# Shared buffers, weights and activations begin at many offsets modulo 512 bytes instead of one

## The chip, the cores and the metric

The kernel runs on one core of a Trainium2 chip (trn2). The metric is the device time of one execution, in microseconds (us). PE is TensorE, DVE VectorE, ACT ScalarE, POOL GpSimd, SP the engine that issues most DMAs; PEld is PE's weight load, which the profile keeps as a row of its own. SBUF is the on-chip memory of 128 partitions; an offset here is a byte offset within a partition, the same in all 128.

## The reference, cut to what matters

Two transformer blocks over 256 positions of width 1024, in float32. The first is a macaron block (feed-forward, mixer of gated linear attention and a gated convolution, feed-forward), the second takes the first one's output, 256 positions of context and a conditioning vector (feed-forward over both, a mixer of a bidirectional mLSTM and a spatial gate, feed-forward).

```python
def first_block(x, ...):
    x = x + 0.5 * swiglu(rmsnorm(x, ffn1_norm[l]), ffn1_w_gate[l], ffn1_w_up[l], ffn1_w_down[l])
    x = x + hybrid_mixer(rmsnorm(x, mix_norm[l]), w_in[l], w_a2[l], b_a[l], gla_out_norm[l], conv_w[l], w_out[l])
    x = x + 0.5 * swiglu(rmsnorm(x, ffn2_norm[l]), ffn2_w_gate[l], ffn2_w_up[l], ffn2_w_down[l])
    return rmsnorm(x, final_norm)

def ffn_sublayer(h, shift, scale, gate, g, w_in, w_out):      # second block
    hn = modulate(rmsnorm_2(h, g), shift, scale)
    a, b = jnp.split(hn @ w_in, 2, axis=-1)
    y = (jax.nn.silu(a) * b) @ w_out
    return h + 0.5 * gate[:, None, :] * y
```

Nearly all of the arithmetic is in the products `hn @ w`: widths 1024 to 2816, some 258 MB of weights read once.

## The kernel before, in words

**Split precision.** A float32 product is made of three products in float32r, a format that PE takes at one column a cycle. Each operand is split into a high part (rounded to float32r, on ACT) and a low part (the rest, on DVE); `mm3` (L142) and `mm3r` (L147) issue high x high, high x low and low x high into one PSUM accumulator. `split` (L116) does it for a weight tile: 512 KB come by DMA into `raw` (4 buffers of 4,096 bytes a partition), ACT writes `wh`, DVE writes `wl` (5 buffers each, pool `wsp`). Activations are normed, transposed by PE against the identity `ident` and split into `XH` and `XL` (16,384 bytes each, pool `const`) by `to_xT` (L175). The hidden activations of a feed-forward (`hT`), values, keys, queries, gates and other long-lived arrays live in 18 shared buffers, S0 to S17 (pool `slots`, tags handed out by `salloc`, L58, and given back by `sfree`); a buffer is as large as its largest tenant, 4,096 or 4,608 bytes.

**The order of the work.** PE follows the program: for each weight tile, all token tiles. In an input projection (`proj_chunk`, L259) the activations XH and XL are the stationary operand (128 columns, 512 bytes, loaded ahead of each product) and the weights wh, wl the moving one (512 columns). In a down projection (`ffn2tok`, L329, `ffn4tok`, L445) the stationary operand is a slice of a shared buffer. Where the result is wanted transposed (`projT`, L307, and `projT2`, L316: the query and key projections, the gate-up projections of the last two feed-forwards) the weights are stationary and XH, XL move, 512 or 256 columns. The first block's query-key projection (L587 to L595) takes its weight tile in slices of 272 and 256 columns; the attention of the second block (L993 to L996) moves values `VH` of 4 heads with 258 columns each, from a shared buffer.

SP issues the loads of the weights in the program's order, some tiles ahead, as far as raw buffers are free; ACT and DVE split as far as wh and wl are free. The modulation vectors of the second block (`ada_gen`, L532) are worked in between by DVE.

**Where things begin.** Pools follow one another in SBUF, and within a pool one tag after the other, each tile's size rounded up to 32 bytes. `pad` (L54) allocates a tile that nothing reads or writes. With the pads of the kernel before (96 elements ahead of `ident`, L1117; 32 after `tri`, L1132; 96 in pool `rp`, L1323) these all begin at 0 modulo 512: ident, XH, XL, the residuals x2 and x3, the temporaries t2, the rows bc, all 18 shared buffers, raw, wh, wl. Every 128-column slice then begins at 0 as well, and every 512- or 256-column slice but those of the two projections with 272 and 258 columns. The small table `cst` begins at 160, `mc` (the modulation sums) at 288, `tri` at 32.

```python
    def salloc(self, shape, dt=F32):
        i = self.free_slots.pop(0)
        ...
            t = self.slots.tile(shape, dt, tag=f"S{i}", name=self.nm(f"S{i}"))
```

Of the kernel before, what the change touches and what calls it, by code (L numbers as in the profile page):

```python
# [14 lines left out]
P = 128  # L15
D = 1024
# [7 lines left out]
class Kern:  # L24
    def __init__(self, tc, A, out, pools):
        self.tc, self.nc, self.A, self.out = tc, tc.nc, A, out
        self.__dict__.update(pools)
        self.n = 0
        self.free_slots = list(range(NSLOT))
        self.slot_of = {}  # L30
        self.filler = None
        self.fill_every = 0
        self.fill_count = 0
        self.filled = 0
        self.pre = []
        self.deferred = []
        self.later_pe = []
        self.held = 0


    def nm(self, s):
# [15 lines left out]

    def salloc(self, shape, dt=F32):  # L58
        i = self.free_slots.pop(0)
        if len(shape) == 3 and shape[1] * shape[2] > D:  # L60
            t = self.slots.tile([P, D + P], dt, tag=f"S{i}", name=self.nm(f"S{i}"))
            t = t[:, :shape[1] * shape[2]].rearrange("p (a b) -> p a b", a=shape[1])
        else:
            t = self.slots.tile(shape, dt, tag=f"S{i}", name=self.nm(f"S{i}"))
        self.slot_of[id(t)] = (i, t)
        return t

# [48 lines left out]
    def split(self, raw, n, dst=None):  # L116
        if dst is not None:
            wh, wl = dst
        else:
            wh = self.wsp.tile([P, 1024], F32R, tag="wh", name=self.nm("wh"))  # L120
            wl = self.wsp.tile([P, 1024], F32R, tag="wl", name=self.nm("wl"))
        if self.held:
            self.held -= 1
            with self.tc.issue_after(self.last[0].ins), self.tc.issue_after(self.last[1].ins):
                self.split_out(wh[:, :n], wl[:, :n], raw[:, :n])
        else:
            self.split_out(wh[:, :n], wl[:, :n], raw[:, :n])
        if self.fill_every:
            self.fill_count += 1
            if self.fill_count % self.fill_every == 0 and next(self.filler, 0) is None:  # L130
                self.filled += 1
        return wh, wl
# [979 lines left out]
    def run(self):  # L1112
# [3 lines left out]
            x[t] = self.xres.tile([P, D], F32, tag=f"x{t}", name=f"x{t}")  # L1116
        self.pad(self.cpool, 96)  # L1117
        self.ident = self.cpool.tile([P, P], F32, tag="ident", name="ident")
        self.XH = self.cpool.tile([P, 8, 512], F32R, tag="XH", name="XH")
        self.XL = self.cpool.tile([P, 8, 512], F32R, tag="XL", name="XL")  # L1120
        make_identity(nc, self.ident)
        g = {"f1": self.bc.tile([P, D], F32, tag="bc", name="bc_f1")}
        pre = []
# [332 lines left out]
```

## Time and profile before

| | us |
|---|---|
| runs before: median of 2 (lowest to highest) | 1410.33 (1409.53 to 1411.13) |
| the profiled execution | 1408.26 |
| its span, first to last instruction | 1406.5 |
| granted TensorE clock, mean | 0.998 of 2.4 GHz |
| PE busy, weight loads busy | 1384.6, 1169.7 |
| DVE, ACT, POOL busy | 919.1, 627.3, 30.4 |

The durations below come from the profiled execution, so a sum is made against 1408.26; the timed runs stand 2 us above it in the median. In a row of PE, `acc<-wh,XH` names the accumulator, the moving operand and the stationary one, in this order; `128x512` is 128 partitions by the moving columns. "Mean ns" of a product is from its start to its end and overlaps with its neighbours; the pace is the distance of the starts. A product of a shared buffer bears the name S without its number.

### The profile page before, as it was taken

Reading aid. Unit: us, or ns where it says so; the run is one execution under the profiler, and the core shown is the slowest. Engines: PE = TensorE matmul, PEld = TensorE weight load, DVE = VectorE, ACT = ScalarE, POOL = GpSimd, SP = SyncE. Lnnn points to the kernel's source line nnn. Section 1 sums busy time; section 2 is a strip of 40 time slices with the busy share of each in tenths; the row PEclk is TensorE's granted clock in tenths of the full one; section 3 lists DMA queues with packets and bytes.
Section 4 is the critical chain, followed back from the end, with each engine's and each line's share of the span. In section 5 each row is a group of like instructions: output and inputs, shape, how many; then the busy total and the mean of one; then the engine's idle time right before and its main releaser. Section 6 shows DMA issues by size and latency. Waiting matters only on the chain. (4 is left out here: it accounts for less than half of the span.)

```text
span 1406.5 us, 18795 instructions
## 1 busy us (share of the span) xinstructions
PE 1384.6 (98%) x7222; PEld 1169.7 (83%) x7222; DVE 919.1 (65%) x1308; ACT 627.3 (45%) x914; POOL 30.4 (2%) x49
## 2 busy tenths in 40 slices
PE   7999999999999999999999999999999999999997
PEld 6778888788888898888888887889888887899986
DVE  6898556878998475543555547377886567655545
ACT  5445447465446442322122224354865455444442
POOL 0000000000000000000000001001010000000000
PEclk9999999999999999999999999999999999999999
DMA  8888646447887664643665543334235666465662
GB/s 287 295 267 280 214 134 218 136 155 269 297 282 255 208 208 139 197 150 103 191 213 179 162 139 104 115 98 148 84 120 192 198 196 217 141 180 184 185 208 69
DMA packets 73307, 260.71 MB, mean 185 GB/s; under 512 B 8172, under 2 KB 9216, under 8 KB 73216
## 3 DMA queue, kind: packets, MB, share of 16 engines
q1 hardware_dynamic: 72928, 259.11, 57.0%
q8 instruction: 57, 0.93, 0.3%
q10 hardware_dynamic: 288, 0.39, 0.1%
q14 instruction: 34, 0.28, 0.1%
HBM read 258.32 MB, written 1.14 MB: 184 GB/s over the span
## 5 line engine op out<-in xcount | busy, mean ns | idle before, releaser
L77 DVE TENSOR_TENSOR wl<-raw,wh 128x1024 fp32r<-128x1024 f32 (+1 forms) x381 | 459.2, 1211 | 319.6 <-ACT wh L74 315.5
L74 ACT ACTIVATE wh<-raw 128x1024 fp32r<-128x1024 f32 (+1 forms) x381 | 398.9, 1051 | 575.7 <-PE acc L87 448.4
L87 PE MATMUL acc<-wh,XH 128*128 128x512 f32 (+2 forms) x816 | 273.6, 393 | 0.5 <-ACT t L74 0.4
L87 PE MATMUL acc<-wl,XH 128*128 128x512 f32 (+2 forms) x816 | 268.9, 388 | 1.5 <-DVE wl L77 1.3
L87 PE MATMUL acc<-wh,XL 128*128 128x512 f32 (+2 forms) x816 | 269.5, 388 | 0.2 <-DVE XL L77 0.2
L87 PE MATMUL acc<-wh,S 128*128 128x512 f32 x872 | 234.2, 391 | 0.2 <-DVE t L80 0.2
L87 PE MATMUL acc<-XH,wh 128*128 128x512 f32 (+1 forms) x776 | 199.7, 337 | 0.0
L87 PE MATMUL acc<-XL,wh 128*128 128x512 f32 (+1 forms) x776 | 199.4, 337 | 0.0
L87 PE MATMUL acc<-XH,wl 128*128 128x512 f32 (+1 forms) x776 | 199.3, 337 | 0.0
L87 PEld LDWEIGHTS acc<-wh,S 128*128 128x128 f32 x872 | 162.8, 188 | 35.7 <-DVE t L80 0.9
L551 DVE SCALAR_TENSOR_TENSOR S<-raw,S 128x1024 f32<-128x1024 f32 x112 | 136.8, 1222 | 68.8 <-DMA raw<-in_w_ada 67.9
L87 PEld LDWEIGHTS acc<-wl,XH 128*128 128x128 f32 x816 | 151.4, 188 | 33.3 <-DVE wl L77 3.9
L87 PEld LDWEIGHTS acc<-wh,XL 128*128 128x128 f32 x816 | 151.8, 188 | 31.1 <-DVE XL L77 1.1
L87 PEld LDWEIGHTS acc<-wh,XH 128*128 128x128 f32 x816 | 151.2, 188 | 30.9 <-ACT t L74 0.6
L87 PEld LDWEIGHTS acc<-XL,wh 128*128 128x128 f32 x776 | 133.8, 190 | 15.3
L87 PEld LDWEIGHTS acc<-XH,wh 128*128 128x128 f32 x776 | 133.7, 190 | 15.4
L87 PEld LDWEIGHTS acc<-XH,wl 128*128 128x128 f32 x776 | 133.8, 190 | 15.3
L87 PE MATMUL acc<-wl,S 128*128 128x512 f32 x436 | 131.5, 389 | 0.0
L87 PEld LDWEIGHTS acc<-wl,S 128*128 128x128 f32 x436 | 81.9, 188 | 16.9
L74 ACT ACTIVATE S<-t 128x512 fp32r<-128x512 f32 (+2 forms) x58 | 31.5, 544 | 48.2 <-DVE t L77 48.2
L74 ACT ACTIVATE XH<-tr 128x512 fp32r<-128x512 f32 x44 | 26.0, 596 | 41.0 <-PE tr L160 40.7
L160 PE MATMUL tr<-ident,t 128*128 128x128 f32 x200 | 32.1, 285 | 10.5 <-DVE t L77 9.4
(165 smaller groups left out, 894.9 us busy)
## 6 DMA issues: line engine op xcount, KB each, us to landing
raw<-in_gu SPq DMA_DIRECT2D x176, 512.0 KB, 4.3
raw<-in_d SPq DMA_DIRECT2D x88, 512.0 KB, 4.3
raw<-in_w_ada SPq DMA_DIRECT2D x72, 512.0 KB, 4.4
raw<-in_w_in SPq DMA_DIRECT2D x68, 512.0 KB, 4.2
raw<-in_w_qk SPq DMA_DIRECT2D x16, 512.0 KB, 3.5
bc<-modd SPq DMA_DIRECT2D x10, 512.0 KB, 4.6
raw<-in_w_out SPq DMA_DIRECT2D x8, 512.0 KB, 3.5
raw<-in_w_b SPq DMA_DIRECT2D x8, 512.0 KB, 4.1
```

The source lines that it names most:

```text
L74: return self.nc.scalar.activation(out=out, in_=in_, func=func, **kw)
L77: return self.nc.vector.tensor_tensor(out=out, in0=a, in1=b, op=op)
L87: self.nc.tensor.matmul(out, l, r, start=start, stop=stop, **kw)
L160: self.nc.tensor.transpose(tr[:, j, :], src[:, j * P:(j + 1) * P], self.ident)
L551: nc.vector.scalar_tensor_tensor(out=junk, in0=raw, scalar=1.0, in1=cb[r], op0=ALU.mult, op1=ALU.mult, accum_out=mc[:, o:o + 1])
```

## The change

Three pads are put around XH and XL in pool `const` (64 elements ahead of XH, 48 ahead of XL, 16 behind it: 256, 192 and 64 bytes, in all 512), one of 8 elements (32 bytes) between the buffers of wh and those of wl, and every shared buffer is allocated as a flat tile of 16 + 1024 or 16 + 1152 elements, of which the tenant takes a view. So XH begins at 256 modulo 512, XL at 448; behind them nothing changes modulo 512 up to the shared buffers; S0 begins at 0 and each next one 64 bytes further (modulo 512), so that the eighteen go twice and a little more round the eight multiples of 64; raw and wh begin at 128, wl at 160. No instruction is added or removed.

```diff
     def salloc(self, shape, dt=F32):
         i = self.free_slots.pop(0)
-        if len(shape) == 3 and shape[1] * shape[2] > D:
-            t = self.slots.tile([P, D + P], dt, tag=f"S{i}", name=self.nm(f"S{i}"))
-            t = t[:, :shape[1] * shape[2]].rearrange("p (a b) -> p a b", a=shape[1])
-        else:
-            t = self.slots.tile(shape, dt, tag=f"S{i}", name=self.nm(f"S{i}"))
+        n = math.prod(shape[1:])
+        t = self.slots.tile([shape[0], 16 + (D if n <= D else D + P)], dt, tag=f"S{i}", name=self.nm(f"S{i}"))[:, :n]
+        if len(shape) == 3:
+            t = t.rearrange("p (a b) -> p a b", a=shape[1])
+        elif len(shape) == 4:
+            t = t.rearrange("p (a b c) -> p a b c", a=shape[1], b=shape[2])
         self.slot_of[id(t)] = (i, t)
         return t
...
             wh = self.wsp.tile([P, 1024], F32R, tag="wh", name=self.nm("wh"))
+            if not self.padded:
+                self.pad(self.wsp, 8)
+                self.padded = True
             wl = self.wsp.tile([P, 1024], F32R, tag="wl", name=self.nm("wl"))
...
         self.pad(self.cpool, 96)
         self.ident = self.cpool.tile([P, P], F32, tag="ident", name="ident")
+        self.pad(self.cpool, 64)
         self.XH = self.cpool.tile([P, 8, 512], F32R, tag="XH", name="XH")
+        self.pad(self.cpool, 48)
         self.XL = self.cpool.tile([P, 8, 512], F32R, tag="XL", name="XL")
+        self.pad(self.cpool, 16)
         make_identity(nc, self.ident)
```

## Rows read from the trace of the kernel before

**Rows 1.** The page: busy time, PE by slices, granted clock by slices
```profile
PE 1384.6 (98%) x7222; PEld 1169.7 (83%) x7222; DVE 919.1 (65%) x1308; ACT 627.3 (45%) x914; POOL 30.4 (2%) x49
...
PE   7999999999999999999999999999999999999997
...
PEclk9999999999999999999999999999999999999999
```

**Rows 2.** Waits: engine, line, releaser: total us, times, longest
```profile
ACT wh L74 <- PE acc L87: 448.4, 185, 9.1
ACT wh L74 <- DMA raw<-in_gu: 104.0, 62, 5.2
PE tr L160 <- DVE t L77: 9.4, 3, 6.9
PEld acc L87 <- DVE wl L77: 3.9, 6, 1.2
PE acc L87 <- DVE wl L77: 1.3, 3, 0.8
```

**Rows 3.** Windows: stretch, length, busy us (count) by engine, clock, DMA share, GB/s
```profile
580.00:840.00 260.00, 260.00 (x1146) 214.45 (x1145) 126.00 (x161) 67.07 (x80) 0.00 (x0) 1.00 0.52 165
1230.00:1336.00 106.00, 106.00 (x885) 106.00 (x885) 56.53 (x75) 49.05 (x74) 0.00 (x0) 1.00 0.60 182
20.00:60.00 40.00, 39.94 (x182) 32.63 (x180) 34.13 (x46) 21.25 (x28) 1.41 (x1) 1.00 0.85 290
60.00:130.00 70.00, 68.55 (x308) 54.95 (x307) 64.15 (x91) 31.75 (x42) 0.00 (x0) 1.00 0.81 265
```

**Rows 4.** PE by shape: moving,stationary, columns, count, busy, mean ns
```profile
L87 PE MATMUL acc<-wh,XH 128*128 128x512 f32 x784 | 267.6, 397 | 0.5 <-ACT t L74 0.4
L87 PE MATMUL tr<-S,S 128*128 128x256 f32 x64 | 14.5, 379 | 0.0
```

**Rows 5.** Weight loads by shape: count, busy us, mean ns, idle before
```profile
L87 PEld LDWEIGHTS acc<-wh,S 128*128 128x128 f32 x872 | 162.8, 188 | 35.7 <-DVE t L80 0.9 <-ACT t L74 0.7 <-DVE t L77 0.7
L87 PEld LDWEIGHTS acc<-XH,wh 128*128 128x128 f32 x776 | 133.7, 190 | 15.4
```

**Rows 6.** Timeline of the gate-up projection, 256 columns: products and their loads
```profile
1230.07 0.40 PE L87 MATMUL acc<-XH,wh 128*128 128x256 f32 x2
...
1229.95 0.31 PEld L87 LDWEIGHTS acc<-XH,wh 128*128 128x128 f32 x2
```

**Rows 7.** Timeline of a 512-column projection: products and their loads
```profile
219.43 0.61 PE L87 MATMUL acc<-wh,XL 128*128 128x512 f32 x2
...
219.21 0.41 PEld L87 LDWEIGHTS acc<-wh,XL 128*128 128x128 f32 x2
```

**Rows 8.** Timeline of PE, query-key projection of the first block
```profile
208.04 0.66 PE L87 MATMUL acc<-wh,XH 128*128 128x272 f32 x4
...
210.02 0.41 PE L87 MATMUL acc<-wh,XL 128*128 128x272 f32 x2
```

**Rows 9.** Timeline of PE, attention products of head 3
```profile
1031.26 0.40 PE L87 MATMUL tr<-S,S 128*128 128x258 f32 x2
...
1033.50 0.28 PE L87 MATMUL tr<-XH,S 128*128 128x256 f32 x1
```

**Rows 10.** PE by shape: transposes out of temporaries and of the modulation table
```profile
L361 PE MATMUL tr<-ident,t 128*128 128x128 f32 x92 | 13.8, 272 | 0.0
L559 PE MATMUL tr<-ident,mc 128*32 128x128 f32 x2 | 0.5, 270 | 0.0
```

**Rows 11.** DVE by shape: one operation, aligned and with an operand off
```profile
L80 DVE SCALAR_TENSOR_TENSOR t<-acc,r,t 128x256 f32<-128x256 f32 x44 | 20.8, 479 | 2.9 <-ACT t L74 2.7
L80 DVE SCALAR_TENSOR_TENSOR t<-acc,cst,t 128x255 f32<-128x255 f32 x16 | 7.7, 479 | 0.1
```

**Rows 12.** DMA issues: count, KB each, median us from issue to landing
```profile
raw<-in_gu SPq DMA_DIRECT2D x176, 512.0 KB, 4.3
```

**Rows 13.** Timeline of PE, plain fp32 products of 256 columns
```profile
1015.41 2.97 PE L87 MATMUL tr<-S,S 128*128 128x256 f32 x13
```

More of the change, by code (lines that the diff above doesn't have):

```diff
@@ L38, in __init__ @@
         self.held = 0
+        self.padded = False
     def nm(self, s):
```

## The prediction

> **What bounds the kernel now.** I read the page first: PE is busy 98% of the span, every slice of its row but the first and the last shows 9, and the clock row shows the full granted clock (2.4 GHz of its two levels) from end to end; DVE is at 65% and ACT at 45% [rows 1]. Then the waits of PE: its longest is 9.4 us, at transposes at the start, and all waits of products for the weight splits come to 1.3 us on PE and 3.9 us on the weight-load row [rows 2]. So the end is set by the pace of 7,222 matmuls. Of them 6,516 are the split-precision products (the rest are transposes and plain fp32 products, two records each); that count is from the program.
>
> The pace is read from stretches with no wait. In 260 us of 512-column products 1,146 start: 226.9 ns each. In 106 us of 256-column products 885 start: 119.8 ns each [rows 3]. The difference, 107.1 ns for 256 columns, is 0.418 ns a column, the full clock. What is left is 226.9 - 213.3 = 13.6 and 119.8 - 106.7 = 13.1 ns: every product pays about 13.3 ns beyond its columns, whatever its width. Summed, 6,516 x 13.3 = 87 us of the span are this fixed part, and 2,919,392 columns / 2.4 GHz = 1,216 us are columns. (The "mean ns" of the groups, 397 for 512 columns and 379 for a plain fp32 product, are latencies that overlap and tell no pace [rows 4].) While a product streams its moving operand, the 128 columns of the next one's stationary operand are loaded: the load of the product that starts at 1230.07 starts at 1229.95, with the product before it [rows 6], and a load's record is 188 to 190 ns long [rows 5]. Two reads of SBUF run side by side, and the change shifts where each begins.
>
> **The change part by part.** No instruction, wait, DMA or queue position is added, removed or moved: pad tiles are never written, and a shared buffer (slot) is the same buffer, made longer by 16 elements and viewed as before. So the sum has only terms of the kind count x change of duration, and I went through who reads or writes a shifted address.
>
> (a) The products. Before, each float32r stationary operand starts at 0 modulo 512 bytes, and so do the moving ones but 132 or so. After, by adding up the pads: XH 256, XL 448, wh 128, wl 160, slot number i 64 x i. The difference "moving start minus start of the stationary operand loaded beside it" becomes 384, 192, 416 and 224 where XH or XL are loaded and weights move; 128, 320, 96 and 288 where weights are loaded; and a mix of all multiples of 32 in the down projections. Only about 124 products keep 0. What a difference costs the trace of before shows in two places only. The query-key projection of the first block has weight slices of 272 and 256 columns, the second one 1,088 bytes in: half of its products have a difference of 64. Its rows start at 208.04 and 210.02 with 4 + 4 + 4 + 4 products between: 123.8 ns each, where (264 mean columns) / 2.4 + 13.3 = 123.3 [rows 8]: no effect (+0.5 ns). The attention products read a value buffer whose heads lie 1,032 bytes apart, so head h moves from offset 8h, in two of three products. Of head 3 (offset 24) 19 products start from 1031.26 up to 1033.50, 117.9 ns each [rows 9], where their 257.3 mean columns give 107.2 + 13.3 = 120.5. That is 2.6 ns less, though from few products of mixed widths. A load that itself starts off 0 is in before only at odd places: transposes out of the modulation table (loads of 32 columns, from 480 and 96) last 270 ns against 272 for the aligned ones [rows 10]; 0 again. So the bounds by the nearest rows are -2.6 and +0.5 ns for a product, with 6,392 products -17 and +3 us. The far ends, since no row has a large difference: the whole fixed part gone (6,392 x -13.3 = -85 us) or paid twice (+85 us). I take 0, the reading with 64, because the new offsets are multiples of 32 and 64 like it and not of 8.
>
> (b) Splits of the weights and of the activations on ACT and DVE, now with buffers at 128, 160 and 64i. The nearest rows are of one DVE operation: 16 with an operand 4 bytes off, 255 columns wide, take 479 ns, as do the aligned ones of 256 [rows 11]: nothing. Cover if that is wrong: from 60 to 130 us DVE is busy 64.2 of 70 us [rows 3], a slack of 5.8 us there and more elsewhere. 10% on DVE would be 6.4 us, so 0.6 us of stall; I put 0.
>
> (c) DMA into raw, now at 128: the weight loads take 4.3 us from issue to landing [rows 12], and no row has such a load at another offset. ACT waits 104 us in 62 waits for these loads and 448 us for a free split buffer [rows 2], but PE waited for the splits only the few us above, so ACT runs ahead of PE. The share of the 16 DMA engines is 0.85 from 20 to 60 us [rows 3]; transfers 15% longer would still fit. 0 taken; beyond 15% the first 60 us would stretch.
>
> (d) Transposes: the identity and the temporaries stay at 0; nothing.
>
> Sum: 1,408.3 us (the profiled execution: span 1,406.5 and 1.8 around it) + 0. The two timed runs have their median 2 us higher, at 1,410.3; I predict 1,410. With the bounds of the nearest rows, and some for (b) and (c), this case by itself spans 1,390 to 1,420.
>
> **The rivals.**
> *Slower: loads that straddle.* Before, each load reads one whole aligned block of 512 bytes. After, 6,254 of 6,516 start off 0 and lie across two (only slots 0, 8 and 16 don't). If such a load pays a second start, of the size of the fixed part, the products it feeds come later: 256-column ones with certainty, since a product starts before the record of its load has ended (two loads from 1229.95, 0.12 apart, take 0.31 us, so one takes 0.19; its product starts at 1230.07) [rows 6]. 512-column ones have cover: two loads from 219.21 take 0.41 us together, so the first, its product 0.23 after the one before, ends at some 219.39, and its product starts at 219.43 [rows 7]. With the cover, some 1,580 x 13.3 = 21 us, 1,431; without it 6,254 x 13.3 = 83 us, 1,493. In between, at half of the wide ones, 1,462. It decides against "no change" from 28 / 6,254 = 4.5 ns a product. For it: no float32r product of before loads from an offset, so nothing shows it free. Against it: these transposes, and the load record has the same length beside either width [rows 5].
> *Faster: equal offsets are what costs 13 ns.* Load and stream start together in the same place of the 512-byte pattern; once apart, the stall goes. For it: 13 plain fp32 products of 256 columns take 2.97 us and the last of them 0.38, so (2.97 - 0.38) / 12 = 216 ns each, two cycles a column (213.3) and 2.5 ns [rows 4, 13]; and head 3 above. If all differences are free, 6,392 x (13.3 - 2.5) = 69 us, 1,341; if half are, 1,375. Against it: 64 keeps the whole 13 ns.
> The Trainium skill, "TensorE: Matmul & The Clock Gate", section "Wait — 56ns, not 53.3ns?", gives back-to-back products 2.5 ns over their columns at full clock. This trace has 13 ns [rows 3], so by that rule something here adds 11 ns that could go: as an estimate from that page 6,392 x 11 = 70 us less. It is this rival, and bears out its price and not its cause.
> *The shift is not what it says:* should the allocator keep the starts (a slot takes the size of its largest tile, and I add 64 bytes to each by its code), nothing changes: 1,410, in the first case.
>
> **How the numbers follow.** No effect of the differences within 2%: 0.50. Straddling or another slow difference by over 2%: 0.32, since no large difference and no shifted load has a row, and the aligned layout leaves only one class that is measured. Faster by over 2%: 0.18. Two per cent, 28 us, is about what a measurement can tell from no change here. The range, 1,374 to 1,468, takes in the first case, the faster one where half of the differences are free, and the straddling one up to a little over its middle; beyond it lie some 0.07 below and 0.1 above.
>
> **What would show it.** Right: 512- and 256-column products still start 227 and 120 ns apart in the same stretches, and load records stay at 188 to 190 ns. Straddling: the query and gate-up projections of the last block (256 columns) slow to 125 ns or more, with longer load records, while wide ones slow less. Equal offsets: paces near 217 and 110 in the classes with weights moving over XH and XL. If classes of one width differ among themselves by their difference, (a) is wrong in its one number; if ACT or DVE rows lengthen or PE waits for splits, (b) or (c) is.

## The result, and the profile after

Changed kernel: 1426.87 us, median of 2 runs (1426.80 and 1426.93), against 1410.33 before: ratio 1.0115, 95% interval 1.0099 to 1.0132. So 16.5 us slower, under two per cent, but clearly more than none. The profiled execution took 1426.8 us where the one before took 1408.26: 18.5 us to account for, and the span grew by 18.4 (1406.5 to 1424.9).

The page of the changed kernel, against [rows 1]:

```profile
PE 1402.8 (98%) x7222; PEld 1168.8 (82%) x7222; DVE 919.2 (65%) x1308; ACT 626.5 (44%) x914; POOL 30.5 (2%) x49
...
PEclk9999999999999999999999999999999999999999
```

The counts of instructions are the same on every engine, the clock row too, and DVE, ACT and POOL are as busy as before to within a microsecond. PE alone has 18.2 us more. Nothing was added, so the products must have become slower. The windows say which (the columns are those of [rows 3]):

```profile
20.00:60.00 40.00, 40.00 (x181) 32.56 (x180) 33.18 (x46) 21.03 (x27) 1.41 (x1) 1.00 0.83 281
60.00:130.00 70.00, 68.83 (x306) 54.66 (x305) 63.68 (x89) 32.31 (x42) 0.00 (x0) 1.00 0.79 264
580.00:840.00 260.00, 260.00 (x1122) 210.12 (x1121) 121.94 (x154) 67.89 (x83) 0.00 (x0) 1.00 0.50 160
1246.00:1334.00 88.00, 88.00 (x747) 88.00 (x746) 46.96 (x62) 42.92 (x64) 0.00 (x0) 1.00 0.63 192
```

From 580 to 840 us 1,122 products start where 1,146 did: 231.7 ns each for 226.9 (512 columns, called *wide* from here). In the gate-up projection with 256 columns (*narrow*) it is 88 / 747 = 117.8 ns, where [rows 3] gave 119.8: these became faster. Summed over the starts of all PE instructions in the two traces, the 4,884 wide products take 1,130.9 us before and 1,151.0 after (+20.1), the 1,608 narrow ones 195.6 and 193.5 (-2.1), and all the rest 64.6 and 65.5 (+1.0). In the mean a wide product loses 4.1 ns and a narrow one wins 1.3 (the expectations below reckon with 4.5 and 1.6).

Nothing that waits or feeds PE changed. By shape, against [rows 4], the transposes of [rows 10], and, on DVE, [rows 11]:

```profile
L89 PE MATMUL acc<-wh,XH 128*128 128x512 f32 x784 | 270.0, 400 | 0.3 <-ACT t L76 0.3
...
L89 PE MATMUL tr<-S,S 128*128 128x256 f32 x64 | 14.5, 379 | 0.0
...
L366 PE MATMUL tr<-ident,t 128*128 128x128 f32 x92 | 13.8, 272 | 0.0
...
L82 DVE SCALAR_TENSOR_TENSOR t<-acc,r,t 128x256 f32<-128x256 f32 x44 | 20.8, 478 | 3.4 <-ACT t L76 3.4
```

The weight loads, against [rows 5]:

```profile
L89 PEld LDWEIGHTS acc<-wh,S 128*128 128x128 f32 x872 | 163.0, 188 | 39.8 <-DVE t L82 1.3 <-ACT t L76 0.5 <-DVE t L79 0.5
...
L89 PEld LDWEIGHTS acc<-XH,wh 128*128 128x128 f32 x776 | 133.4, 189 | 17.1
```

The waits, against [rows 2]:

```profile
ACT wh L76 <- PE acc L89: 465.9, 189, 9.3
...
PE tr L165 <- DVE t L79: 10.4, 4, 6.5
...
PEld acc L89 <- DVE wl L79: 3.4, 6, 1.0
...
PE acc L89 <- DVE wl L79: 1.0, 2, 0.5
```

And the weight DMA (issues, KB each, us from issue to landing), against [rows 12]:

```profile
raw<-in_gu SPq DMA_DIRECT2D x176, 512.0 KB, 4.4
```

Loads are as long as before though most of them now begin off a block, PE waits for the splits as little as before (1.0 and 3.4 us), a weight DMA lands in 4.4 us for 4.3, and a plain fp32 product still takes 379 ns. ACT waits 17.5 us more for buffers, because PE gives them back later. Only the float32r products with 512 columns are slower: the group shown went from 397 to 400 ns a record, and in the window above the starts came 4.8 ns further apart.

### The profile page after: what moved, and what is told of

It is laid out like the page before. It is cut to its first block, busy times and chain, and to the rows that moved or that the text cites. A ratio compares the mean times of both kernels' runs of the same rounds, so it can differ in the third digit from the quotient of the medians.

```text
span 1424.9 us, 18798 instructions
## 1 busy us (share of the span) xinstructions
PE 1402.8 (98%) x7222; PEld 1168.8 (82%) x7222; DVE 919.2 (65%) x1308; ACT 626.5 (44%) x914; POOL 30.5 (2%) x49
## 5 line engine op out<-in xcount | busy, mean ns | idle before, releaser
L89 PE MATMUL acc<-wl,XH 128*128 128x512 f32 (+2 forms) x816 | 272.8, 392 | 1.2 <-DVE wl L79 1.0
L89 PE MATMUL acc<-wh,S 128*128 128x512 f32 x872 | 237.6, 395 | 0.7 <-DVE t L82 0.7
```

The costliest lines, as they stand in the source:

```text
L89: self.nc.tensor.matmul(out, l, r, start=start, stop=stop, **kw)
```

## The experiments

What changed in the programs are starting offsets, so all theories are about them. By the first, the *difference* counts: the start of the moving operand minus the start of the stationary operand that is loaded beside it (that of the next product). By the second, a load that straddles two 512-byte blocks costs, or an absolute start does. A third had DVE or ACT in the way. (In every stage in which one difference holds throughout, a product's own stationary operand begins where the next one's does, modulo 256; so no run here tells which of the two counts.) In the figures below a wide or a narrow pace is the distance of starts in the trace, and differences are given modulo 256, for the reason that the second group shows. All these kernels compute the whole output. "Before" was run again beside each group: 1411.51, 1410.12, 1411.06 and 1409.94 us in the four.

### Does the start count, or the difference?

Everything at 128 (XH, XL, the shared buffers, raw, wh, wl): every load straddles, every difference stays 0.

```diff
+        self.pad(self.cpool, 32)
         self.XH = self.cpool.tile([P, 8, 512], F32R, tag="XH", name="XH")
         self.XL = self.cpool.tile([P, 8, 512], F32R, tag="XL", name="XL")
+        self.cpool.tile([P, 96], F32, tag="padx", name="padx")
...
-            k.pad(rp, 96)
+            k.pad(rp, 128)
```

> XH, XL, all shared buffers, raw, wh and wl begin at 128 modulo 512: every float32r product keeps a difference of 0, but no operand begins at 0. The changed kernel lost 4.5 ns on each of 4,884 products of 512 columns and won 1.6 ns on each of some 1,600 narrow ones. Theory absolute start (it matters where an operand begins, not the difference): the same again, 231 to 232 ns and 118 ns, about +19 us, 1,430. Theory difference: 226.7 and 120 ns, 1,410. Theory mixing (cost only where offsets change from one product to the next): 1,410.

Only wh and wl at 128, all else at 0: half of the operands straddle, every product has the difference 128.

```diff
+            if not self.padded:
+                self.pad(self.wsp, 32)
+                self.padded = True
             wh = self.wsp.tile([P, 1024], F32R, tag="wh", name=self.nm("wh"))
```

> Only wh and wl begin at 128; XH, XL and the shared buffers at 0. Absolute start of the moving operand: the 3,660 wide products with weights moving slow to 231 to 232, the 1,176 wide ones with weights loaded stay at 226.7, narrow ones (weights loaded) at 120: +16 us, 1,427. Absolute start of the loaded operand: the other way round, only weights-loaded products change, 1,176 x 4.5 - 1,152 x 1.6 = +3.5 us, 1,414. Difference: both kinds, +20 us, 1,430. Mixing: 1,410.

The first took 1410.82 us, ratio 1.0003 [0.9988, 1.0018]; the second 1429.35, ratio 1.0132 [1.0117, 1.0147]. The kernel before, in a wide and a narrow window:

```profile
600.00:830.00 230.00, 230.00 (x1014) 189.59 (x1013) 106.66 (x135) 59.75 (x71) 0.00 (x0) 1.00 0.51 160
1246.00:1334.00 88.00, 88.00 (x736) 88.00 (x735) 46.83 (x62) 41.88 (x63) 0.00 (x0) 1.00 0.59 182
```

The same with everything at 128:

```profile
600.00:830.00 230.00, 230.00 (x1014) 189.61 (x1013) 107.39 (x136) 58.63 (x70) 0.00 (x0) 1.00 0.51 162
1246.00:1334.00 88.00, 88.00 (x735) 88.00 (x735) 45.38 (x60) 40.45 (x60) 0.00 (x0) 1.00 0.60 185
```

And one of its groups of weight loads:

```profile
L87 PEld LDWEIGHTS acc<-XH,wh 128*128 128x128 f32 x776 | 133.7, 190 | 15.3
```

The same windows with the weights alone at 128:

```profile
600.00:830.00 230.00, 230.00 (x989) 185.46 (x988) 107.17 (x137) 58.99 (x71) 0.00 (x0) 1.00 0.50 158
1246.00:1334.00 88.00, 88.00 (x744) 88.00 (x743) 47.53 (x63) 41.95 (x62) 0.00 (x0) 1.00 0.62 194
```

With all loads straddling, 230 us hold 1,014 products (226.8 ns), as many as before, and a load takes 190 ns: straddling costs nothing, nor does a start of 128 bytes that all operands share. With a difference of 128 they hold 989 (232.6 ns). This falls alike on products that load the weights and on those that move them (both 232.4 to 232.6, start to start). Beside a DVE or ACT instruction and beside none it is also the same (232.3 to 232.6 in all four classes), so the third theory falls too.

The Trainium skill, "SBUF — State Buffer", section "Who interferes with whom", gives PE two independent read ports, one for the moving operand and one for weight loads, and says that PE never waits on anyone. The trace agrees as to DVE and ACT: the four classes just named lie within 0.3 ns. Of the two reads of PE itself it can't be the whole story: moving one against the other by 128 bytes costs 5.8 ns a wide product here, and the measurement decides.

### Modulo what?

XH and XL at 256, all else at 0:

```diff
+        self.pad(self.cpool, 64)
         self.XH = self.cpool.tile([P, 8, 512], F32R, tag="XH", name="XH")
         self.XL = self.cpool.tile([P, 8, 512], F32R, tag="XL", name="XL")
+        self.cpool.tile([P, 64], F32, tag="padx", name="padx")
```

> Only XH and XL begin at 256. Absolute start of the moving operand: the products with XH or XL moving change (1,224 wide x 4.5 less 1,340 narrow x 1.6), +3.5 us, 1,414; the 2,352 gate-up and projection products with XH or XL loaded stay at 226.7. Loaded operand: those 2,352 slow to 231 to 232, +10.5 us, 1,421. Difference: both, +14 us, 1,424. Mixing: 1,410. The down projections (shared buffer loaded, weights moving, all at 0) stay at 226.7 in every theory but one in which the place of another buffer matters.

1411.12 us, ratio 0.9999 [0.9990, 1.0009], with 1,014 products in 600 to 830 us, the number before. A second run had XH and wl at 256 and XL, wh and the shared buffers at 0, so that differences of 0 and 256 stand mixed in all stages:

```diff
             wh = self.wsp.tile([P, 1024], F32R, tag="wh", name=self.nm("wh"))
+            if not self.padded:
+                self.pad(self.wsp, 64)
+                self.padded = True
             wl = self.wsp.tile([P, 1024], F32R, tag="wl", name=self.nm("wl"))
...
+        self.pad(self.cpool, 64)
         self.XH = self.cpool.tile([P, 8, 512], F32R, tag="XH", name="XH")
+        self.cpool.tile([P, 64], F32, tag="padx", name="padx")
         self.XL = self.cpool.tile([P, 8, 512], F32R, tag="XL", name="XL")
```

> XH and wl begin at 256, XL, wh, the shared buffers at 0: differences of 0 and 256 follow one another in every group of three products. Theory difference modulo 256: 226.7 and 120 ns throughout, 1,411. Theory modulo 512, or cost of any change of the difference from product to product: over 1,420.

1410.40 us, ratio 1.0003 [0.9994, 1.0012], 1,013 products. So 256 is like 0, mixed with it too.

### What does each difference cost?

First the offset of wh and wl changed with every weight tile (0, 8, 16, 32, 64, 128, 192, 256 bytes in turn), in one run:

```diff
+            o = (0, 2, 4, 8, 16, 32, 48, 64)[self.turn % 8]
+            self.turn += 1
-            wh = self.wsp.tile([P, 1024], F32R, tag="wh", name=self.nm("wh"))
+            wh = self.wsp.tile([P, 1088], F32R, tag="wh", name=self.nm("wh"))[:, o:o + 1024]
-            wl = self.wsp.tile([P, 1024], F32R, tag="wl", name=self.nm("wl"))
+            wl = self.wsp.tile([P, 1088], F32R, tag="wl", name=self.nm("wl"))[:, o:o + 1024]
```

> Each weight tile begins at another offset (0, 8, 16, 32, 64, 128, 192, 256 bytes in turn, and the same plus 256 in every other buffer), XH, XL and the shared buffers at 0. By the trace, class by class: absolute start of the moving operand: 231 to 232 ns for every tile off 0 in the stages where weights move, 226.7 where it is at 0, and nothing where weights are loaded. Loaded operand: the reverse. Difference: both. Mixing: classes differ little among themselves, all a little over 226.7 where the tile changes. About 1,420 to 1,430 in the first and third, 1,410 to 1,415 else.

1424.84 us. Where the weights move, wide paces came out at 228.4 with difference 0, 229.5 with 64, 231.9 with 128, 231.8 with 16, and 233.1 to 234.0 with 8, 32 and 192; narrow ones at 119.8 with 0, 116.0 with 192 and 123.3 with 248. Even the products with difference 0 read 1.7 ns high here, beside neighbours with other offsets. So next the offset was held for six tiles in turn:

```diff
-            o = (0, 2, 4, 8, 16, 32, 48, 64)[self.turn % 8]
+            o = (0, 8, 24, 32, 40, 48, 56, 60)[self.turn // 6 % 8]
```

> The offset of the weight tiles changes only after every sixth tile (0, 32, 96, 128, 160, 192, 224, 240 bytes, all with or without 256), so inside a block every product has one difference and mixing is away. By the trace, class by class: theory difference modulo 256 with uniform neighbours: weights moving at 0: 226.7, 128: 232.4, 192: about 233; narrow with weights loaded: 120 at 0, 119 at 128, near 114 at -64; what 96, 160, 224 and 240 give is open: if a difference below 226.7 exists for wide products, it shows here. Theory of the sweep without neighbours: the same numbers as there, 229 to 234 everywhere off 0.

1427.63 us in its one run. A block is read from the starts of two of its products in the timeline (a window's count is no use for short blocks: it takes in the products still running at its edge). The pairs below are, in time order, from blocks with difference 64, 32, 16, 240, 0 and then, narrow, 32 and 0:

```profile
581.27 0.62 PE L88 MATMUL acc<-XL,wh 128*128 128x512 f32 x2
...
602.33 0.62 PE L88 MATMUL acc<-XH,wl 128*128 128x512 f32 x2
602.79 0.63 PE L88 MATMUL acc<-XH,wh 128*128 128x512 f32 x2
...
635.92 0.62 PE L88 MATMUL acc<-XH,wl 128*128 128x512 f32 x2
636.38 0.61 PE L88 MATMUL acc<-XH,wh 128*128 128x512 f32 x2
...
646.81 0.62 PE L88 MATMUL acc<-XH,wl 128*128 128x512 f32 x2
...
649.00 0.64 PE L88 MATMUL acc<-wl,S 128*128 128x512 f32 x2
...
670.05 0.62 PE L88 MATMUL acc<-wh,S 128*128 128x512 f32 x2
...
947.69 0.61 PE L88 MATMUL acc<-XH,wl 128*128 128x512 f32 x2
...
969.91 0.62 PE L88 MATMUL acc<-XH,wh 128*128 128x512 f32 x2
...
1258.70 0.40 PE L88 MATMUL acc<-XH,wl 128*128 128x256 f32 x2
...
1270.13 0.39 PE L88 MATMUL acc<-XH,wh 128*128 128x256 f32 x2
...
1292.61 0.40 PE L88 MATMUL acc<-XH,wl 128*128 128x256 f32 x2
...
1304.37 0.40 PE L88 MATMUL acc<-XH,wh 128*128 128x256 f32 x2
```

Between the starts of the pairs lie 92, 142, 46, 89, 98, 98 and 98 products. So difference 64 gives 21.06 / 92 = 228.9 ns; 32 gives 33.13 / 142 = 233.3; 16 gives 226.7; 240 gives 236.5; 0 gives 226.7; narrow 32 gives 116.6 and narrow 0 gives 120.0. Blocks of 24 or more products alike read so:

| difference mod 256 | 0 | 32 | 64 | 96 | 128 | 160 | 192 | 224 | 240 |
|---|---|---|---|---|---|---|---|---|---|
| wide, ns | 226.7 | 233.3 | 228.9 | 233.3 | 232.4-233.3 | 234.2 | 233.4 | 233.3 | 236-237, but 226.7 and 233.3 in one block each |
| narrow, ns | 119.9 | 116.7 | 117.8 | - | 118.6 | 117.4 | - | 118.3 | - |

Where a difference occurs with weights moving and with weights loaded the paces agree (32: 233.4 and 233.3; 160: 234.2 and 234.3; 128: 232.4 to 233.3 and 232.4), but for 16, below.

One difference can have several paces. Of seven blocks with difference 240, all with weights moving, five read 236 to 237 ns, one 226.7 and one 233.3. The block with 226.7, the one right behind it, and the one with 233.3:

```profile
424.44 0.61 PE L88 MATMUL acc<-wh,XL 128*128 128x512 f32 x2
...
431.69 0.62 PE L88 MATMUL acc<-wl,XH 128*128 128x512 f32 x2
...
433.05 0.40 PE L88 MATMUL acc<-wh,XL 128*128 128x512 f32 x1
...
440.62 0.64 PE L88 MATMUL acc<-wl,XH 128*128 128x512 f32 x2
...
1121.03 0.39 PE L88 MATMUL acc<-wl,XH 128*128 128x512 f32 x1
...
1137.13 0.63 PE L88 MATMUL acc<-wl,XH 128*128 128x512 f32 x2
```

Between the starts of these pairs lie 32, 32 and 69 products: 226.6, 236.6 and 233.3 ns. The starts modulo 256 and the columns are alike in the three, so the difference alone does not set the pace. What else does, no run here isolates.

Finer offsets, 4 to 48 bytes, in the same blocks:

```diff
-            o = (0, 8, 24, 32, 40, 48, 56, 60)[self.turn // 6 % 8]
+            o = (1, 2, 3, 4, 5, 6, 10, 12)[self.turn // 6 % 8]
```

> As the kernel with blocks of six weight tiles, with offsets of 4, 8, 12, 16, 20, 24, 40 and 48 bytes. Theory that equal starts are a special lucky place of a 256-byte pattern: wide products at 229 to 235 ns for all offsets but 16 moving-minus-loaded, which had 226.7 in the blocks; nothing below 226.7; about 1,425 us. Rival, equal starts are only one of several places and a finer step finds a cheaper one: some class of 512-column products below 225 ns.

1434.23 us in one run, the slowest of all. A block with difference 20, in the timeline:

```profile
1069.60 0.63 PE L88 MATMUL acc<-wh,XH 128*128 128x512 f32 x2
...
1086.76 0.40 PE L88 MATMUL acc<-wh,XH 128*128 128x512 f32 x1
```

72 products in 17.16 us are 238.3 ns each; other blocks of this difference read 236.0 to 240.0. Difference 4 gave 236.5 to 237.0, 12 gave 228.8 to 230.0, 8, 24, 40 and 48 gave 233.0 to 233.9 in all blocks but two (234.8 and 235.0), and 16 gave 231.7, where the run before it had 226.7. There wh and wl were loaded, from 240; here they move, from 16. With the weights loaded the differences 208 to 252 gave 230.0 to 233.3, among them 240 with 233.3. So the difference alone does not say everything at such small steps. No wide block read below 226.7.

### Can the narrow gain be had alone?

Weights at 64 in the whole kernel, then only where products are narrow (last feed-forward's gate-up, second block's queries and keys), where the weights are loaded and the difference becomes -64, that is 192.

```diff
+            if not self.padded:
+                self.pad(self.wsp, 16)
+                self.padded = True
             wh = self.wsp.tile([P, 1024], F32R, tag="wh", name=self.nm("wh"))
```

> Only wh and wl begin at 64, all else at 0: weights moving means a difference of 64, weights loaded one of 192 (modulo 256). Theory difference modulo 256, with the classes of the sweep: 3,660 wide products at 229.5 (+2.8 each), 1,176 wide ones with weights loaded at 229.8 (+3.1), 1,152 narrow ones at 116 (-4): +9 us, 1,420, half of what the shift by 128 cost. Theory that any difference but 0 and 256 costs the same 5.7 ns: +20 us, 1,430.

```diff
+            o = self.off
-            wh = self.wsp.tile([P, 1024], F32R, tag="wh", name=self.nm("wh"))
+            wh = self.wsp.tile([P, 1088], F32R, tag="wh", name=self.nm("wh"))[:, o:o + 1024]
-            wl = self.wsp.tile([P, 1024], F32R, tag="wl", name=self.nm("wl"))
+            wl = self.wsp.tile([P, 1088], F32R, tag="wl", name=self.nm("wl"))[:, o:o + 1024]
...
+                self.off = 16
                 ws = [self.unit(Wgu[2 * f + j]) for j in range(2)]
+                self.off = 0
...
```

> As before, but the weight tiles of the two stages with 256-column products of XH and XL (the query projection of the second block and the gate-up of the last feed-forward, 1,152 products) begin at 64 or 320, so their difference is 192 or 448. Theory difference modulo 256: the sweep has 115.9 and 116.2 ns there, where a difference of 0 has 119.8; 1,152 x -3.8 = -4.4 us, 1,407, faster than both kernels, ratio 0.997. Rival: the short starts in the sweep were paid back by neighbours of other differences; then nothing, 1,411.

Weights at 64 everywhere: 1416.56 us, ratio 1.0046 [1.0032, 1.0059]. Windows:

```profile
600.00:830.00 230.00, 230.00 (x992) 185.58 (x991) 108.95 (x137) 59.99 (x73) 0.00 (x0) 1.00 0.50 159
1246.00:1334.00 88.00, 88.00 (x779) 88.00 (x778) 48.45 (x64) 44.00 (x65) 0.00 (x0) 1.00 0.64 194
```

Only in the narrow stages: 1402.89 us, ratio 0.9956 [0.9943, 0.9969], faster than both kernels. Windows:

```profile
600.00:830.00 230.00, 230.00 (x1014) 189.59 (x1013) 106.43 (x135) 59.59 (x71) 0.00 (x0) 1.00 0.50 160
1236.00:1326.00 90.00, 90.00 (x797) 90.00 (x796) 49.55 (x66) 43.90 (x66) 0.00 (x0) 1.00 0.64 195
```

In the narrow stage the pace is 90 / 797 = 112.9 ns for 119.8 (by starts, 113.3), while the wide one stays at 226.8. Some 1,150 products x 6.6 ns are 7.6 us; 7.2 were gained. With the weights at 64 everywhere the same narrow gain is there (88 / 779 = 113.0), but 1,176 wide products that load weights go to 233.3 (+7.8 us) and the 3,660 that move them, at difference 64, to 229.1 (+8.8): net +9 by this sum, +6.4 measured.

### The parts of the change

Each part of the change alone, and the change without one. The pad between wh and wl alone (32 bytes):

```diff
             wh = self.wsp.tile([P, 1024], F32R, tag="wh", name=self.nm("wh"))
+            if not self.padded:
+                self.pad(self.wsp, 8)
+                self.padded = True
             wl = self.wsp.tile([P, 1024], F32R, tag="wl", name=self.nm("wl"))
```

> Only the pad of 32 bytes between the buffers of wh and wl, one part of the change: a third of the products (wl moving: +32; wl loaded: -32) get a difference, two thirds keep 0. Theory that each product pays for its own difference: 1,220 wide products x 6.4 + 392 wide ones x 4.2 - a third of a us = +9 us, 1,420; products of wh stay at 226.7. Theory mixing on top (a stall shifts the start of the next products, so those with difference 0 pay too): all three of a group slow, up to +25 us, 1,435.

The shared buffers at 64 x i alone (with raw, wh and wl put back to 0):

```diff
+        t = self.slots.tile([shape[0], 16 + (D if n <= D else D + P)], dt, tag=f"S{i}", name=self.nm(f"S{i}"))[:, :n]
...
+        if not self.padded:
+            self.pad(self.raw, 96)
+            self.padded = True
         raw = self.raw.tile([P, 1024], F32, tag="raw", name=self.nm("raw"))
```

> Only the shared buffers are made longer and begin at 64 i; XH, XL, raw, wh, wl stay at 0: the down projections (1,308 wide products) get mixed differences of multiples of 64, the gate-up ones keep 0. Theory difference with mixing: 231 to 232 in the down projections, 226.7 elsewhere: +6 us, 1,417. Rival: the shared buffers are also written and read by ACT and DVE, whose rows would lengthen: more than that, and waits of PE.

The pads around XH and XL alone:

```diff
+        self.pad(self.cpool, 64)
         self.XH = self.cpool.tile([P, 8, 512], F32R, tag="XH", name="XH")
+        self.pad(self.cpool, 48)
         self.XL = self.cpool.tile([P, 8, 512], F32R, tag="XL", name="XL")
+        self.pad(self.cpool, 16)
```

> Only the pads around XH (256) and XL (448); weights and shared buffers at 0. Differences: 0 beside XH loaded, 64 beside XL loaded (2,352 wide), 0 and 192 with XH and XL moving (1,224 wide, 1,152 narrow). Theory difference with mixing: 229 to 231 in the gate-up projections, 231 with XH, XL moving wide, 118 narrow; down projections at 226.7: +12 us, 1,423. Theory each for itself: only the third with XL pays: +5 us, 1,416.

The whole change without the pad between wh and wl (against the changed kernel):

```diff
             wh = self.wsp.tile([P, 1024], F32R, tag="wh", name=self.nm("wh"))
-            if not self.padded:
-                self.pad(self.wsp, 8)
-                self.padded = True
             wl = self.wsp.tile([P, 1024], F32R, tag="wl", name=self.nm("wl"))
```

> The changed kernel without the pad of 32 bytes between wh and wl: wh and wl at 128, XH 256, XL 448, shared buffers at 64 i. No wide class has a difference of 0 or 256 but in the down projections. Theory difference with mixing (a product that is off costs 3 to 7 ns whatever the mix): 1,425, within 3 us of the changed kernel, though the same pad by itself cost 17 us. Theory that the parts add: 17 us less, 1,410.

| | us | ratio [95%] | over its before |
|---|---|---|---|
| wl pad alone | 1427.01 | 1.0118 [1.0102, 1.0133] | +16.9 |
| shared buffers alone | 1416.57 | 1.0042 [1.0027, 1.0057] | +5.5 |
| XH, XL pads alone | 1419.90 | 1.0066 [1.0049, 1.0083] | +8.8 |
| change without the wl pad | 1424.55 | 1.0101 [1.0086, 1.0116] | +13.5 |
| the change | 1426.87 | 1.0115 [1.0099, 1.0132] | +16.5 |

The parts don't add. Alone the first three sum to 31.2 us. A fourth part has no row here: the longer shared buffers move wh and wl to 128, and this alone, the second run of the first group, cost 17.8. The four would make some 49 us; together they cost 16.5. The reason shows in the first. With only wl shifted, two of three products keep difference 0, and yet the window that takes in both kinds reads nearly as slow as with all weights at 128 (992 products, where that run had 989). The wide window of the wl pad alone:

```profile
600.00:830.00 230.00, 230.00 (x992) 185.51 (x990) 107.04 (x136) 59.03 (x71) 0.00 (x0) 1.00 0.50 159
```

By class, moving wl at difference 32 takes 233.6 to 234.1 ns, and moving wh at difference 0 beside it 230.6 to 231.2 instead of 226.7. With the XH and XL pads alone, products with difference 0 next to others average 230.6 (weights loaded) and 231.7 (XH or XL loaded). A shifted product makes its neighbours pay; once a stage is mixed, a further shift adds little. And where all products keep 0 the pace is untouched: with the pads of XH and XL alone the down projections stay at 227.1, with the shared buffers alone the narrow window holds 736 in 88 us.

## Why the prediction was wrong

It forecast no change, at 1,410 us; the time is 1,426.9, above the 1,390 to 1,420 that this case allowed itself. That it lies inside the wide range of 1,374 to 1,468, and less than 2% from no change, is luck: the range was made that wide for the straddling and the faster rival, and neither came as described. And two per cent was too coarse a line. The text called 28 us about what a measurement can tell from no change; the interval of the ratio, 1.0099 to 1.0132, is some 5 us wide. The frame was right: the end is set by the pace of the products, the difference of two starts is the quantity that the change touches, and no instruction, wait or queue moved.

**(a), the products, is the step that failed**, in its one number: "I take 0, the reading with 64". Two things were wrong with carrying that reading.

- It was taken on slices of 272 and 256 columns, half of them at difference 0 [rows 8], and head 3 on 257 [rows 9]. The effect depends on the width, and has the other sign there. Narrow products mostly gain (117.8 for 119.9 in the narrow block at 64, 113.3 at 192; at 16 they stayed at 119.9, and with difference 232 one stretch read 121.8 and the next 118.7), wide ones, three quarters of all, pay (228.9 at 64, 233 at most others). The -2.6 ns of head 3, which the text weighed as a few products of mixed widths, had the sign of the narrow class.
- 64 is not like the other multiples of 32. In wide blocks it costs 2.2 ns, the least of them; 128 costs 5.7 to 6.6, and 32, 96, 160, 192 and 224 cost 6.6 to 7.5. Both bounds, -2.6 and +0.5 ns, came from narrow products; the changed kernel pays 4.1 for a wide one in the mean, 4.8 in the window from 580 to 840 us.

The term, as measured: 4,884 wide products +20.1 us, 1,608 narrow ones -2.1, where 0 stood. (One reading ahead of the sum was off, and nothing hangs on it: the 9.4 us called PE's longest wait are the total of three, the longest of them 6.9 [rows 2].)

**(b), (c) and (d) held:** ACT and DVE groups, the landing of the weights and the transposes are as before, and PE waits no longer than before for the splits.

**The slower rival** had the sign of the total and not the mechanism. It made loads pay for straddling, narrow products surely, wide ones behind cover, with longer load records. Measured: all loads straddling cost nothing, load records stay at 188 to 190 ns, and wide products pay while narrow ones gain.

**The faster rival** (equal offsets cost the 13 ns) fell for wide products: none got below 226.7. For narrow ones it was half right: 13.3 ns over the columns became 6.6 at difference 192 (113.3 - 106.7), not 2.5, and this is what the fastest kernel here uses (1402.89 us).

**The shift is not what it says** fell: with the difference in the program as counted from the pads, paces follow it class by class.

The text's own test, "if classes of one width differ among themselves by their difference, (a) is wrong in its one number", is what came.

## What to carry to other kernels

A layout shift adds no instruction and may still move the pace of every product: where PE is the bound, compare the starts of moving and stationary operands, and keep wide (512-column) float32r products at equal starts modulo 256 bytes, all of a stage alike. For narrow ones (256 columns), try an offset: 64 bytes on the loaded weights gave some 5% of that stage here. And a reading of "no effect" holds for the size it was taken on: before it is carried to products of another width, ask whether a row of that width exists, and if none does, let the range and not the value say so.

## What the runs showed that was not expected

- The two widths go opposite ways with the same offset: at difference 192, 226.7 to 233.4 ns wide, 120.0 to 113.3 narrow.
- Four steady paces are multiples of 16 cycles of 2.4 GHz: 226.7 ns is 544, that is 512 columns and 32; 120.0 is 288, or 256 and 32; 233.3 is 560 (512 and 48); 113.3 is 272 (256 and 16). The 13 ns that every product of before paid are these 32 cycles. Other paces are means of distances that differ from product to product: with the weights at 128 single distances alternate between 238 and 229 ns for long stretches, though all differences are alike.
- One difference, 240, ran at 226.7, 233.3 and 236 to 237 ns in different blocks of one execution.
- 16 reads 226.7 with the weights loaded from 240 and 231.7 with the weights moving from 16.

Why the starts of PE's two reads matter like this, with this period and these values, stays open: the runs show on what the pace depends, not the mechanism, and that the reads collide in SBUF is not shown. Other steps of 4 bytes, and narrow products over shifted shared buffers as the stationary operand, were not tried by themselves.
